# A layer's up-projection with part and remainder of x as one 512-column operand, and its products taken out of PSUM first

## The chip, the core and the metric

The kernel runs on one core of a Trainium2 chip. The metric is device time of one execution in microseconds (us); before the change it is 472.7 us, the median of three runs (472.5 to 473.08). The engines are named as the profile names them: PE is TensorE (PEld its weight loads), DVE is VectorE, ACT is ScalarE, POOL is GpSimd, SP is SyncE. PE writes its products to PSUM, from where DVE and ACT read them; everything else lives in SBUF.

## The reference

One layer (256 positions, width 1024, float32) of a mixer and a gated MLP, with a LayerNorm after each. The change touches the MLP alone, 2 x 2816 channels wide:

```python
def conv_ffn_sublayer(x, w_up, w_ffn_conv, b_ffn_conv, w_down):
    u = causal_dwconv(x @ w_up, w_ffn_conv) + b_ffn_conv
    gate, val = jnp.split(u, 2, axis=-1)
    return (jax.nn.silu(gate) * val) @ w_down

x = layer_norm(DN_ALPHA * x + mix, ln1_g, ln1_b)
ffn = conv_ffn_sublayer(x, w_up, w_ffn_conv, b_ffn_conv, w_down)
x = layer_norm(DN_ALPHA * x + ffn, ln2_g, ln2_b)
```

`causal_dwconv` is y_t = w_0 u_t + w_1 u_(t-1) + w_2 u_(t-2), channel by channel.

## The kernel before

**Products in three.** Every float32 operand of a product is split in two (`split`, L164): ACT casts it to the type in which PE multiplies (the part, `h`), DVE subtracts the part from the source (the remainder, `l`). `mm3` (L227) then makes a product of three matmuls, part by part, part by remainder and remainder by part, all summed in one PSUM tile.

**Weights as pieces.** Weights arrive in blocks of 1 MB (63 of them, `blocks`), DMAs on SP into three `raw` buffers. `prep` (L137) splits the next piece of a block, 128 x 512, into a pair (`h`, `l`) of the 61 `b2` buffers; a block is four pieces. A piece may be split as long as it is less than `LEAD` = 10 pieces beyond those that products have used up (`used`). After each group of products comes `tick(n)` (L174): it counts the `n` pieces used up, runs what was put on the list `late`, splits up to `n` + 1 pieces, then runs the group's `consume`, then one entry of the list `side`.

**The up-projection.** `project` (L238) makes two tiles of 128 channels by 256 positions from four pieces: 8 steps of the contraction, each an `mm3`, into one of three PSUM tiles named `acc` (another five are named `att`). The weights are the stationary operand, `x1Th` and `x1Tl` (part and remainder of x, turned) the moving one, 256 columns. What follows a tile is in `hidden` (L703): `taps` (L697) runs on the PSUM tile itself, first tap and bias on ACT (L699), the other two taps on DVE (L701), two instructions of which the second needs the first. For a gate tile a SiLU on ACT (L710) is put on `late`; for a value tile DVE multiplies with the gate (L714), and the split of the result into `h` and `l` is put on `late`.

**The loop.** The first pair of channel blocks (j = 0) is projected with x as the stationary operand (L734 takes it out of PSUM); `first_up` (L740), four times on `side`, turns it on PE (L743) into `att` tiles and gives it to the same `gate` and `value`; its result is `h0`. Then j = 2, 4, ..., 20 each project two gate tiles (called A and B below) and two value tiles (C and D), which are 8 pieces, and from j = 4 on also run the down-projection of the pair before, 4 pieces; j = 4 runs two, that of `h0` first. One down-projection is 18 matmuls of 512 columns and 12 of 256 (`sums`, L631: two tiles of 512 for the first 128 positions; one of 512 and two of 256 for the others).

The engines run their instructions in the order of the built program, which a scheduler makes of the order in the code.

Of the kernel before, what the change touches and what calls it, by code (L numbers as in the profile page):

```python
# [28 lines left out]
GATE = 5376  # L29

RAW = 3
LEAD = 10
B2 = 61
WARM = 6

# [2 lines left out]
def trunk(ctx: ExitStack, tc, x, w_in, w_short_conv, w_moba_proj, w_dil_proj, w_conv_proj, w_mix_out,  # L38
# [18 lines left out]
    def buf(dt=F32, shape=(P, 512)):  # L57
        return act.tile(list(shape), dt, tag="b2", name=fresh("b"), bufs=B2)

    def acc(shape=(P, 512)):  # L60
        return ps.tile(list(shape), F32, tag="acc", name=fresh("acc"), bufs=3)
# [52 lines left out]
            block(kview(w_down, 0, D, i, i + 2))  # L114

    loads, pieces, ready, loading = [], [], [], [None]
    used = [0]

    def load_next(between=None):
        i = len(loads)  # L120
# [16 lines left out]
    def prep(n=1):  # L137

        for _ in range(n):
            i = len(ready)  # L140
            if i >= min(len(pieces), used[0] + LEAD):
                return
            r, c, last = pieces[i]
            h, l = buf(F32R), buf(F32R)
            split(r[:, c:c + 512], h, l)
            ready.append((h, l))
            if last:
                load_next()

    def take(n):  # L150

        i = used[0]
        assert len(ready) >= i + n, (len(ready), i, n)
        return ready[i:i + n]
# [19 lines left out]
    def tick(n, consume=None, ahead=1):  # L174


        used[0] += n
        while late:
            late.pop(0)()
        prep(n + ahead)  # L180
        if consume:
            consume()
        if side:
            side.pop(0)()
# [27 lines left out]
    nc.gpsimd.iota(diff, pattern=[[-1, P]], base=0, channel_multiplier=1)  # L212
    nc.vector.tensor_scalar(ident, diff, 0.0, None, op0=OP.is_equal)

    xTh = act.tile([P, KT, T], F32R, tag="xTh", name="xTh")
    xTl = act.tile([P, KT, T], F32R, tag="xTl", name="xTl")

    def transpose_x(k, k1):
        p = att((P, k1 - k, T))
# [13 lines left out]
    def cut(w, k, c0, c1):  # L233

        c = (k % 2) * 256
        return [t[:, c + c0:c + c1] for t in w[k // 2]]

    def project(consume, xh=xTh, xl=xTl, ahead=1):  # L238

        w = take(4)  # L240
        for c in range(2):
            o = acc((P, T))
            for k in range(KT):
                mm3(o, *cut(w, k, c * P, c * P + P), xh[:, k, :], xl[:, k, :], k == 0, k == KT - 1)
            tick(2, lambda: consume(c, o), ahead)

    def by_tokens(xs, n, consume, ahead=1):

# [405 lines left out]


    x1 = act.tile([P, 2, D], F32, tag="xs", name="x1", bufs=2)
    x1Th = act.tile([P, KT, T], F32R, tag="xTh", name="x1Th")
    x1Tl = act.tile([P, KT, T], F32R, tag="xTl", name="x1Tl")

    def turn_x1(t, half):  # L660
        p = acc((P, 4, P))
# [41 lines left out]
    def hidden(j):  # L703
# [12 lines left out]

        return gate, value, (h, l)

    while len(ready) < used[0] + 8:
        prep()  # L720
    w = take(8)
# [18 lines left out]
    def first_up(i, c):  # L740
        o = att((P, T))
        for t in range(2):
            nc.tensor.transpose(o[:, t * P:(t + 1) * P], u[t][:, (2 * i + c) * P:(2 * i + c + 1) * P], ident)  # L743
        (gate0, value0)[i](c, o)

    side += [lambda i=i, c=c: first_up(i, c) for i in range(2) for c in range(2)]
    dn = sums()
    pend = [h0]
    for j in range(2, NJ, 2):
        gate, value, h = hidden(j)  # L750
        project(gate, x1Th, x1Tl)
        project(value, x1Th, x1Tl)
        while 2 < j < NJ - 2 and pend:
            w = take(4)
            for t in range(2):
                if t and j == NJ - 4:
                    held = (pend[0], w)
                    tick(2)
                    break
                for c0, c1, p in dn[t]:  # L760
                    for k in range(2):
                        row_products(p, pend[0], w, k, t, c0, c1, pend[0] is h0 and k == 0, False)
                tick(2)
            pend.pop(0)
        pend.append(h)
# [38 lines left out]
```

## Time and profile before

| | us |
|---|---|
| median of 3 runs | 472.7 |
| profiled execution | 472.95 |
| its span, first to last instruction | 471.2 |
| PE busy | 460.7 (98%) |
| DVE busy | 355.5 (75%) |
| ACT busy | 268.2 (57%) |

Busy time says whether an instruction was under way; matmuls overlap, each lasting longer than the distance to the next, so PE's rate is read from the starts of successive rows in the timeline. The same holds on DVE and ACT in a smaller degree: where instructions follow without waits, they start closer together than each lasts. The stage of the change is the last 185 us or so of the span, from 287 us.

### The profile page before, as it was taken

Reading aid. Unit: us, or ns where it says so; the run is one execution under the profiler, and the core shown is the slowest. Engines: PE = TensorE matmul, PEld = TensorE weight load, DVE = VectorE, ACT = ScalarE, POOL = GpSimd, SP = SyncE. Lnnn points to the kernel's source line nnn. Section 1 sums busy time; section 2 is a strip of 40 time slices with the busy share of each in tenths; the row PEclk is TensorE's granted clock in tenths of the full one; section 3 lists DMA queues with packets and bytes.
Section 4 is the critical chain, followed back from the end, with each engine's and each line's share of the span. In section 5 each row is a group of like instructions: output and inputs, shape, how many; then the busy total and the mean of one; then the engine's idle time right before and its main releaser. Section 6 shows DMA issues by size and latency. Waiting matters only on the chain.

```text
span 471.2 us, 8149 instructions
## 1 busy us (share of the span) xinstructions
PE 460.7 (98%) x3095; PEld 423.9 (90%) x3095; DVE 355.5 (75%) x756; ACT 268.2 (57%) x568; POOL 10.4 (2%) x29
## 2 busy tenths in 40 slices
PE   7999999999999999999999999999999999999993
PEld 5999898999999888888888899999999999999983
DVE  5899996868989844964487966997676786786866
ACT  3896773837577745534455235875565564664710
POOL 1100000010100000000000000000000000000000
PEclk9999999999999999999999999999999999999998
DMA  8975647354453746645664705457545636636202
GB/s 278 307 228 180 211 147 234 126 177 133 137 179 98 232 162 222 209 128 200 224 210 125 246 1 196 162 180 268 182 176 184 215 138 222 223 100 253 99 1 89
DMA packets 57738, 83.45 MB, mean 177 GB/s; under 512 B 1704, under 2 KB 41316, under 8 KB 57700
## 3 DMA queue, kind: packets, MB, share of 16 engines
q1 hardware_dynamic: 57700, 82.94, 53.0%
q8 instruction: 24, 0.39, 0.3%
q14 instruction: 14, 0.11, 0.1%
HBM read 81.89 MB, written 1.05 MB: 176 GB/s over the span
## 4 chain that ended last, share of the span: by engine, by line
PE 95%; DVE 2%; DMA 1%; issue 0%; SPq 0%; ACT 0%; DVEq 0%
PE acc L229 23%; PE acc L231 23%; PE acc L230 23%; PE att L229 7%; PE att L230 7%; PE att L231 7%; PE att L326 2%; PE att L347 1%; DMA xs<-in_x_dram 1%; PE acc L499 1%; PE att L499 1%; DVE b L169 1%; DVE b L298 0%; PE att L587 0%; PE att L222 0%
## 5 line engine op out<-in xcount | busy, mean ns | idle before, releaser
L169 DVE TENSOR_TENSOR b<-raw,b 128x512 fp32r<-128x512 f32 x300 | 193.9, 686 | 40.8 <-ACT b L168 38.7
L168 ACT CAST b<-raw 128x512 fp32r<-128x512 f32 x288 | 160.1, 618 | 2.4 <-DMA raw<-in_w_up_dram 2.1
L229 PE MATMUL acc<-x1Th,b 128*128 128x256 f32 x320 | 90.9, 284 | 0.0
L231 PE MATMUL acc<-x1Th,b 128*128 128x256 f32 x320 | 90.6, 283 | 0.0
L230 PE MATMUL acc<-x1Tl,b 128*128 128x256 f32 x320 | 90.5, 283 | 0.0
L229 PE MATMUL acc<-xTh,b 128*128 128x256 f32 x224 | 63.8, 285 | 0.4 <-DVE b L298 0.4
L231 PE MATMUL acc<-xTh,b 128*128 128x256 f32 x224 | 63.4, 283 | 0.0
L230 PE MATMUL acc<-xTl,b 128*128 128x256 f32 x224 | 63.4, 283 | 0.0
L230 PEld LDWEIGHTS acc<-x1Tl,b 128*128 128x128 f32 x320 | 61.4, 192 | 0.1
L229 PEld LDWEIGHTS acc<-x1Th,b 128*128 128x128 f32 x320 | 61.4, 192 | 0.1
L231 PEld LDWEIGHTS acc<-x1Th,b 128*128 128x128 f32 x320 | 61.4, 192 | 0.0
L701 DVE SCALAR_TENSOR_TENSOR b<-acc,fconv,b 128x255 f32<-128x255 f32 x80 | 38.4, 480 | 30.3 <-ACT b L699 29.3
L229 PE MATMUL att<-b,b 128*128 128x512 f32 (+1 forms) x170 | 59.1, 348 | 0.0
L230 PE MATMUL att<-b,b 128*128 128x512 f32 (+1 forms) x170 | 58.9, 346 | 0.0
L231 PE MATMUL att<-b,b 128*128 128x512 f32 (+1 forms) x170 | 58.7, 346 | 0.0
L229 PE MATMUL acc<-b,xTh 128*128 128x512 f32 (+1 forms) x144 | 54.8, 382 | 0.0
L230 PE MATMUL acc<-b,xTh 128*128 128x512 f32 (+1 forms) x144 | 54.4, 378 | 0.0
L231 PE MATMUL acc<-b,xTl 128*128 128x512 f32 (+1 forms) x144 | 54.4, 378 | 0.0
L229 PEld LDWEIGHTS acc<-xTh,b 128*128 128x128 f32 x224 | 42.9, 192 | 0.7 <-PE acc L231 0.6
L230 PEld LDWEIGHTS acc<-xTl,b 128*128 128x128 f32 x224 | 43.0, 192 | 0.0
L231 PEld LDWEIGHTS acc<-xTh,b 128*128 128x128 f32 x224 | 42.9, 192 | 0.0
L699 ACT ACTIVATE b<-acc,fconv 128x256 f32<-128x256 f32 x40 | 22.5, 563 | 28.6 <-PE acc L231 28.5
(118 smaller groups left out, 646.6 us busy)
## 6 DMA issues: line engine op xcount, KB each, us to landing
raw<-in_w_in_dram SPq DMA_DIRECT2D x30, 1024.0 KB, 5.4
raw<-in_w_up_dram SPq DMA_DIRECT2D x22, 1024.0 KB, 5.2
raw<-in_w_down_dram SPq DMA_DIRECT2D x11, 1024.0 KB, 5.0
raw<-in_w_mix_out_dram SPq DMA_DIRECT2D x4, 1024.0 KB, 4.8
raw<-in_w_in_dram SPq DMA_DIRECT2D x12, 256.0 KB, 5.7
raw<-in_w_conv_proj_dram SPq DMA_DIRECT2D x4, 512.0 KB, 4.8
raw<-in_w_moba_proj_dram SPq DMA_DIRECT2D x4, 512.0 KB, 5.7
xs<-in_x_dram SPq DMA_DIRECT2D x4, 256.0 KB, 5.6
```

The source lines that it names most:

```text
L168: nc.scalar.copy(h, src)
L169: nc.vector.tensor_sub(l, src, h.bitcast(F32))
L229: nc.tensor.matmul(o, ah, bh, start=first, stop=False)
L230: nc.tensor.matmul(o, ah, bl, start=False, stop=False)
L231: nc.tensor.matmul(o, al, bh, start=False, stop=last)
L326: nc.tensor.matmul(o, qt, k[i][:, a, :], start=i == 0, stop=i == 1)
L347: nc.tensor.transpose(p[:, i, :], b, ident)
L499: last = nc.tensor.matmul(o[c], w[i][:, c * P:c * P + P], xt[:, k, :], start=k + part == 0, stop=k == KT - 1 and i == 1)
L699: nc.scalar.activation(v, o, AF.Identity, bias=w[3], scale=w[0])
L701: nc.vector.scalar_tensor_tensor(v[:, j:], o[:, :T - j], w[j], v[:, j:], op0=OP.mult, op1=OP.add)
```

## The change

The tiles of part and remainder of x become one tile, `xT` (`x1T`), in which the 256 columns of each step's part are followed by the 256 of its remainder. For j = 2 to 20 `project_wide` takes the place of `project`: it multiplies the weights' part with all 512 columns in one matmul, and the weights' remainder with x's part (256 columns) into the right half of the same PSUM tile. The two halves are then summed by `summed`: ACT copies the right half to SBUF, DVE adds the left half. `taps` gets that sum in SBUF in place of the PSUM tile. In `project_wide` a tile's `consume` comes ahead of `tick`, not inside it. The lead becomes 14 pieces from the first up-projection on, and the four `first_up` on `side` are put apart by empty entries.

```diff
--- before.py
+++ after.py
@@ -29,7 +29,6 @@
 GATE = 5376
 
 RAW = 3
-LEAD = 10
 B2 = 61
 WARM = 6
 
@@ -114,7 +113,7 @@
             block(kview(w_down, 0, D, i, i + 2))
 
     loads, pieces, ready, loading = [], [], [], [None]
-    used = [0]
+    used, lead = [0], [10]
 
     def load_next(between=None):
         i = len(loads)
@@ -138,7 +137,7 @@
 
         for _ in range(n):
             i = len(ready)
-            if i >= min(len(pieces), used[0] + LEAD):
+            if i >= min(len(pieces), used[0] + lead[0]):
                 return
             r, c, last = pieces[i]
             h, l = buf(F32R), buf(F32R)
@@ -212,8 +211,8 @@
     nc.gpsimd.iota(diff, pattern=[[-1, P]], base=0, channel_multiplier=1)
     nc.vector.tensor_scalar(ident, diff, 0.0, None, op0=OP.is_equal)
 
-    xTh = act.tile([P, KT, T], F32R, tag="xTh", name="xTh")
-    xTl = act.tile([P, KT, T], F32R, tag="xTl", name="xTl")
+    xT = act.tile([P, KT, 2, T], F32R, tag="xT", name="xT")
+    xTh, xTl = xT[:, :, 0, :], xT[:, :, 1, :]
 
     def transpose_x(k, k1):
         p = att((P, k1 - k, T))
@@ -243,6 +242,26 @@
             for k in range(KT):
                 mm3(o, *cut(w, k, c * P, c * P + P), xh[:, k, :], xl[:, k, :], k == 0, k == KT - 1)
             tick(2, lambda: consume(c, o), ahead)
+
+    def project_wide(consume, xT):
+
+
+        w = take(4)
+        for c in range(2):
+            o = acc((P, 2, T))
+            f = o.rearrange("p a t -> p (a t)")
+            for k in range(KT):
+                wh, wl = cut(w, k, c * P, c * P + P)
+                nc.tensor.matmul(f, wh, xT[:, k, :, :].rearrange("p a t -> p (a t)"), start=k == 0, stop=False)
+                nc.tensor.matmul(o[:, 1, :], wl, xT[:, k, 0, :], start=False, stop=k == KT - 1)
+            consume(c, o)
+            tick(2)
+
+    def summed(o):
+        s = buf(F32, (P, T))
+        nc.scalar.copy(s, o[:, 1, :])
+        nc.vector.tensor_add(s, o[:, 0, :], s)
+        return s
 
     def by_tokens(xs, n, consume, ahead=1):
 
@@ -654,8 +673,8 @@
 
 
     x1 = act.tile([P, 2, D], F32, tag="xs", name="x1", bufs=2)
-    x1Th = act.tile([P, KT, T], F32R, tag="xTh", name="x1Th")
-    x1Tl = act.tile([P, KT, T], F32R, tag="xTl", name="x1Tl")
+    x1T = act.tile([P, KT, 2, T], F32R, tag="xT", name="x1T")
+    x1Th, x1Tl = x1T[:, :, 0, :], x1T[:, :, 1, :]
 
     def turn_x1(t, half):
         p = acc((P, 4, P))
@@ -716,6 +735,7 @@
 
         return gate, value, (h, l)
 
+    lead[0] = 14
     while len(ready) < used[0] + 8:
         prep()
     w = take(8)
@@ -743,13 +763,15 @@
             nc.tensor.transpose(o[:, t * P:(t + 1) * P], u[t][:, (2 * i + c) * P:(2 * i + c + 1) * P], ident)
         (gate0, value0)[i](c, o)
 
-    side += [lambda i=i, c=c: first_up(i, c) for i in range(2) for c in range(2)]
+    for i in range(2):
+        for c in range(2):
+            side += [lambda i=i, c=c: first_up(i, c), lambda: None]
     dn = sums()
     pend = [h0]
     for j in range(2, NJ, 2):
         gate, value, h = hidden(j)
-        project(gate, x1Th, x1Tl)
-        project(value, x1Th, x1Tl)
+        project_wide(lambda c, o: gate(c, summed(o)), x1T)
+        project_wide(lambda c, o: value(c, summed(o)), x1T)
         while 2 < j < NJ - 2 and pend:
             w = take(4)
             for t in range(2):
```

Line numbers below are those of each kernel; L228 to L230 and L167, L168 after the change are L229 to L231 and L168, L169 before it, L718 and L720 are L699 and L701, L729 is L710 and L733 is L714.

PE, the first three steps of the contraction in a tile of the up-projection (tile A of j = 2; `b679` and `b683` are parts of weights, `b680` and `b684` remainders). Before:

```order
L229 MATMUL acc725_3489<-x1Th_3065,b679_3225 128x256
L230 MATMUL acc725_3489<-x1Tl_3066,b679_3225 128x256
L231 MATMUL acc725_3489<-x1Th_3065,b680_3226 128x256
L229 MATMUL acc725_3489<-x1Th_3065,b679_3225 128x256
L230 MATMUL acc725_3489<-x1Tl_3066,b679_3225 128x256
L231 MATMUL acc725_3489<-x1Th_3065,b680_3226 128x256
L229 MATMUL acc725_3489<-x1Th_3065,b683_3284 128x256
L230 MATMUL acc725_3489<-x1Tl_3066,b683_3284 128x256
L231 MATMUL acc725_3489<-x1Th_3065,b684_3285 128x256
```

After:

```order
L255 MATMUL acc730_3497<-x1T_3064,b679_3223 128x512
L256 MATMUL acc730_3497<-x1T_3064,b680_3224 128x256
L255 MATMUL acc730_3497<-x1T_3064,b679_3223 128x512
L256 MATMUL acc730_3497<-x1T_3064,b680_3224 128x256
L255 MATMUL acc730_3497<-x1T_3064,b683_3282 128x512
L256 MATMUL acc730_3497<-x1T_3064,b684_3283 128x256
```

Of each three matmuls the first two, which have the same weights, have become one of 512 columns.

DVE, j = 2, from the last pieces ahead of tile A on (`b726` is the gate's buffer of j = 2, `b717` that of j = 0; L168 with `raw` is a piece). Before:

```order
L169 TENSOR_TENSOR b727_3515<-raw678_3223,b726_3514 128x512
L169 TENSOR_TENSOR b729_3519<-raw678_3223,b728_3518 128x512
L701 SCALAR_TENSOR_TENSOR b721_3485<-acc725_3489,fconv_113,b721_3485 128x255
L701 SCALAR_TENSOR_TENSOR b712_3476<-att731_3527,fconv_113,b712_3476 128x255
L701 SCALAR_TENSOR_TENSOR b721_3485<-acc725_3489,fconv_113,b721_3485 128x254
L701 SCALAR_TENSOR_TENSOR b712_3476<-att731_3527,fconv_113,b712_3476 128x254
L169 TENSOR_TENSOR b734_3561<-raw696_3397,b733_3560 128x512
L701 SCALAR_TENSOR_TENSOR b721_3485<-acc732_3533,fconv_113,b721_3485 128x255
L701 SCALAR_TENSOR_TENSOR b721_3485<-acc732_3533,fconv_113,b721_3485 128x254
L169 TENSOR_TENSOR b736_3565<-raw696_3397,b735_3564 128x512
L701 SCALAR_TENSOR_TENSOR b712_3476<-att737_3571,fconv_113,b712_3476 128x255
L701 SCALAR_TENSOR_TENSOR b712_3476<-att737_3571,fconv_113,b712_3476 128x254
```

After:

```order
L168 TENSOR_TENSOR b715_3479<-raw678_3221,b714_3478 128x512
L263 TENSOR_TENSOR b731_3514<-acc730_3497,b731_3514 128x256
L720 SCALAR_TENSOR_TENSOR b726_3493<-b731_3514,fconv_112,b726_3493 128x255
L720 SCALAR_TENSOR_TENSOR b726_3493<-b731_3514,fconv_112,b726_3493 128x254
L168 TENSOR_TENSOR b733_3522<-raw696_3395,b732_3521 128x512
L168 TENSOR_TENSOR b735_3526<-raw696_3395,b734_3525 128x512
L168 TENSOR_TENSOR b737_3530<-raw696_3395,b736_3529 128x512
L720 SCALAR_TENSOR_TENSOR b717_3484<-att738_3533,fconv_112,b717_3484 128x255
L263 TENSOR_TENSOR b740_3556<-acc739_3539,b740_3556 128x256
L720 SCALAR_TENSOR_TENSOR b717_3484<-att738_3533,fconv_112,b717_3484 128x254
L168 TENSOR_TENSOR b742_3565<-raw696_3395,b741_3564 128x512
L720 SCALAR_TENSOR_TENSOR b726_3493<-b740_3556,fconv_112,b726_3493 128x255
```

An addition (L263) stands ahead of each tile's two taps, the taps read its result, and three pieces follow tile A where one did. From the first piece after the wait at 288.40 us in the trace to the product (L733) that completes the first half of `h0`'s values, DVE's list now holds 44 instructions: 17 pieces, 6 additions, 17 taps, 2 products and 2 subtractions of results.

ACT, a later j, tile A to the silu of B (the gate's buffer is `b900` before and `b929` after). Before:

```order
L699 ACTIVATE b900_4557<-acc904_4561,fconv_113 128x256
L168 CAST b911_4625<-raw885_4462 128x512
L168 CAST b913_4629<-raw885_4462 128x512
L168 CAST b916_4662<-raw885_4462 128x512
L710 ACTIVATE b900_4557<-b900_4557 128x256
L699 ACTIVATE b900_4557<-acc910_4599,fconv_113 128x256
L168 CAST b918_4666<-raw885_4462 128x512
```

After:

```order
L262 COPY b934_4494<-acc933_4477 128x256
L718 ACTIVATE b929_4473<-b934_4494,fconv_112 128x256
L167 CAST b935_4501<-raw900_4321 128x512
L167 CAST b937_4505<-raw900_4321 128x512
L729 ACTIVATE b929_4473<-b929_4473 128x256
L262 COPY b941_4528<-acc940_4511 128x256
L167 CAST b942_4535<-raw913_4389 128x512
L718 ACTIVATE b929_4473<-b941_4528,fconv_112 128x256
L167 CAST b944_4539<-raw913_4389 128x512
L262 COPY b947_4560<-acc946_4543 128x256
L729 ACTIVATE b929_4473<-b929_4473 128x256
```

The copies out of PSUM (L262) are new and stand ahead of the pieces; the first tap (L718) of a tile stands behind its copy and, by what it reads, behind DVE's addition.

## Rows read from the trace of the kernel before

**Rows 1.** The page: span, and busy time of each engine.

```profile
span 471.2 us, 8149 instructions
PE 460.7 (98%) x3095; PEld 423.9 (90%) x3095; DVE 355.5 (75%) x756; ACT 268.2 (57%) x568; POOL 10.4 (2%) x29
```

**Rows 2.** The page: chain that ended last, by engine.

```profile
PE 95%; DVE 2%; DMA 1%; issue 0%; SPq 0%; ACT 0%; DVEq 0%
```

**Rows 3.** Windows: busy us (count) per engine, clock, DMA; start and a later j.

```profile
298.00:303.00 5.00, 5.00 (x44) 5.00 (x43) 5.00 (x14) 3.98 (x10) 0.00 (x0) 1.00 0.57 181
353.00:370.00 17.00, 17.00 (x128) 16.28 (x127) 12.45 (x25) 9.96 (x21) 0.00 (x0) 1.00 0.55 186
```

**Rows 4.** Groups by shape: PE, up-projection; count, busy us, mean ns, idle before.

```profile
L229 PE MATMUL acc<-x1Th,b 128*128 128x256 f32 x320 | 90.9, 284 | 0.0
```

**Rows 5.** Timeline, PE: start us, length us; first of j = 2, then 64 starts.

```profile
287.06 0.28 PE L229 MATMUL acc<-x1Th,b 128*128 128x256 f32 x1
...
299.82 0.28 PE L230 MATMUL acc<-x1Tl,b 128*128 128x256 f32 x1
...
307.50 0.28 PE L231 MATMUL acc<-x1Th,b 128*128 128x256 f32 x1
```

**Rows 6.** Timeline, PE: first and last of 204 matmuls of 512 columns.

```profile
158.33 0.40 PE L229 MATMUL acc<-b,xTh 128*128 128x512 f32 x1
...
204.51 0.40 PE L231 MATMUL acc<-b,xTl 128*128 128x512 f32 x1
```

**Rows 7.** Timeline, PE: eight of 512 columns between 256s (first of down-projection).

```profile
307.62 0.40 PE L229 MATMUL att<-b,b 128*128 128x512 f32 x1
307.85 0.40 PE L230 MATMUL att<-b,b 128*128 128x512 f32 x1
...
309.23 0.39 PE L230 MATMUL att<-b,b 128*128 128x512 f32 x1
309.46 0.28 PE L229 MATMUL acc<-x1Th,b 128*128 128x256 f32 x1
309.57 0.28 PE L230 MATMUL acc<-x1Tl,b 128*128 128x256 f32 x1
```

**Rows 8.** Timeline, DVE, start of the stage: start, length, [idle before].

```profile
288.40 3.70 DVE L169 TENSOR_TENSOR b<-raw,b 128x512 fp32r<-128x512 f32 x6 [3.99 <-ACT b L168]
292.02 0.48 DVE L701 SCALAR_TENSOR_TENSOR b<-acc,fconv,b 128x255 f32<-128x255 f32 x1
292.41 0.48 DVE L701 SCALAR_TENSOR_TENSOR b<-att,fconv,b 128x255 f32<-128x255 f32 x1
...
294.18 1.00 DVE L701 SCALAR_TENSOR_TENSOR b<-acc,fconv,b 128x255 f32<-128x255 f32 x2
296.26 0.69 DVE L169 TENSOR_TENSOR b<-raw,b 128x512 fp32r<-128x512 f32 x1 [1.08 <-ACT b L168]
...
300.55 0.75 DVE L714 TENSOR_TENSOR b<-b,b 128x256 f32<-128x256 f32 x2
...
306.86 0.42 DVE L169 TENSOR_TENSOR b<-b,b 128x256 fp32r<-128x256 f32 x1
```

**Rows 9.** Timeline, ACT, the same stretch.

```profile
290.87 0.56 ACT L699 ACTIVATE b<-acc,fconv 128x256 f32<-128x256 f32 x1
...
293.70 1.28 ACT L710 ACT_TABLE_LOAD   x1
```

**Rows 10.** Groups by shape: the nearest instructions to the added ones.

```profile
L541 ACT COPY b<-acc 128x256 f32<-128x256 f32 x4 | 1.5, 371 | 1.9 <-PE acc L231 1.9
L544 DVE TENSOR_TENSOR b<-acc,b 128x256 f32<-128x256 f32 x4 | 1.7, 420 | 1.0 <-PE acc L231 1.0
L548 DVE SCALAR_TENSOR_TENSOR b<-b,sconv,b 128x255 f32<-128x255 f32 x4 | 1.9, 484 | 0.1
L168 ACT CAST b<-b 128x256 fp32r<-128x256 f32 x26 | 10.5, 407 | 24.5 <-DVE b L714 20.8 <-DVE b L567 3.6
L168 ACT CAST b<-att 128x256 fp32r<-128x256 f32 x14 | 5.3, 377 | 23.6 <-PE att L587 21.6 <-DVE b L169 2.0
```

## Prediction

> **What bounds the kernel now.** I read the page first: PE is busy for 460.7 of the span's 471.2 us [rows 1], and the chain that ended last is PE's for 95%, with 2% for DVE [rows 2]. So the time is what PE's queue takes, plus any wait that is put into it. Then the windows, because DVE's 75% is an average [rows 1, 3]: in a later j DVE works 12.45 of 17 us, but between 298 and 303 us 5.00 of 5.00, at the start of the very stage that the change touches. TensorE's granted clock stands at 1.00 in both, its upper level, 2.4 GHz; I expect it to stay there. Last the timelines of PE, DVE and ACT, for what an instruction occupies. In the groups a matmul of 256 columns lasts 284 ns [rows 4], but successive ones start closer, and only the distance between starts can be saved.
>
> **The pair of matmuls (gain).** 64 starts of 256-column matmuls lie between 299.82 and 307.50 us: 7.68 us / 64 = 120 ns each [rows 5]. 203 starts of 512 columns lie between 158.33 and 204.51 us: 46.18 / 203 = 227.5 ns [rows 6]. Twice the columns cost 107.5 ns more, so some 12.5 ns of each matmul do not depend on its width, and those are saved with the matmul that goes. Three of 256 take 360 ns; one of 512 and one of 256 take 347.5. There are 320 such threes [rows 4]: 320 x 12.5 ns = 4.0 us. The alternation of widths is not in the trace for long. At the changes of width a 512 behind a 256 takes 0.23 us and a 256 behind a 512 0.11 [rows 7]; so the pair may be anything from 340 to 355 ns, the gain from 6.4 to 1.6 us. I take 4.0, from the long runs.
>
> The trace's fixed part can be weighed against a rule. The Trainium skill, "TensorE: Matmul & The Clock Gate", section "Back-to-back issue gap", gives N / 2.4 + 2.5 ns between warm matmuls: 109.2 ns for 256 columns and 215.8 for 512, an estimate from that page. By that rule the change would save 2.5 ns per three, 0.8 us in all. The trace does not agree: 120 and 227.5 ns at a clock of 1.00.
>
> **What is added on ACT and DVE.** Per tile one ACT copy from PSUM, 0.37 us by the same operation and shape in the mixer, and one DVE addition with a PSUM operand, 0.42 by the multiplication of that shape [rows 10]; 40 tiles, so 15 and 17 us of work. The taps on DVE then read SBUF: 484 ns [rows 10] against 0.48 now [rows 8], nothing. The first tap on ACT reads SBUF in place of PSUM: 0.56 [rows 9] plus the 30 ns by which casts of this shape differ [rows 10], 0.59; bounds 0.56 and 0.65. None of it is on PE. It costs time only where PE waits for DVE or ACT, and there are two such places to look at.
>
> **A later j (cover holds).** PE needs four tiles of 8 x 0.3475 = 2.78 us and a down-projection of 18 x 0.2275 + 12 x 0.12 = 5.54 us: 16.66 us a period, against 17.06 now. DVE occupies, from starts that follow without a wait [rows 8]: a piece (3.70 - 0.69) / 5 = 0.60, a tap 0.39, any other instruction of 256 columns 0.33. Twelve pieces 7.2, eight taps 3.1, four additions 1.3, two products and two subtractions 1.3: 12.9 us. To that come waits inside the chain, which the new order leaves bare at tiles A and C: the addition, then ACT's tap, then DVE's tap is 0.42 + 0.59 + two hand-overs of 0.04 (the two dependent taps take 1.00 us, 2 x 0.48 and 0.04 [rows 8]) = 1.09 in place of 0.33, twice 0.76; at B a piece covers all but 0.16; four instructions that wait for DVE's own result, 0.13 each; the cast of C's result, 0.58, and the cast of the piece behind it, 0.18. Together 3.0: 15.9 us. DVE fits under PE with 0.7 us to spare per period, 4%. So I cost the additions at nothing here; the cover is PE's period, and without it each j costs the excess. A piece is split 14 ahead of use, over one period of 12, and a PSUM tile is waited for only when DVE is three tiles late, so a delay of a few us is not felt at once.
>
> **The first two j (cover gone).** Here `h0`'s chain and the silu's table load come on top, and PE does not have a down-projection to give DVE time. Now DVE works from 288.40 us on [rows 8]; the last subtraction for `h0` ends at 306.86 + 0.42 = 307.28, and PE starts the first eight matmuls that need it at 307.62 [rows 7]. The margin is 0.3 us. After the change DVE has, from the same start to the product that completes the first half of `h0`, 17 pieces x 0.60 + 6 additions x 0.33 + 17 taps x 0.39 + 4 others x 0.33 = 20.2 us; the lead of 14 alone brings three of these pieces forward. The waits: the table load, 1.28 long [rows 9] and 1.08 of DVE's idle time now [rows 8], 1.2; two bare turns over ACT, 1.5; one cast turn 0.6 and the piece behind it 0.2; four own results 0.5; second waits 0.2. That is 24.4 us, so that product starts at 312.8; with its own 0.42, ACT's cast of 0.41 [rows 10] and two hand-overs the down-projection of j = 4 can start at 313.7. PE, from 287.06 [rows 5], would be there after eight tiles and the four turns of `first_up` (now 7 x 2.88 us and 0.4 up to 307.62): 287.06 + 22.24 + 0.4 = 309.7. So PE waits 4.0 us. About half falls already ahead of tile C of j = 4, which takes the PSUM tile that D of j = 2 must leave: the 29 instructions of DVE's list up to the addition for D, 13 of them pieces, take 13.7 us and waits of 4.0, to 306.1; PE is there at 287.06 + 6 x 2.78 + 0.4 = 304.1. Bounds: none of the waits on ACT left bare, 20.2 us, gives no wait on PE at all; every instruction at its full length (0.69, 0.42, 0.48) gives 28 us with the waits, 8 us of waiting.
>
> At the end one more copy and addition lie ahead of the last hidden values, behind 18 matmuls (4.1 us) of other work against a chain of some 3.7: 0, at most 0.7; I take 0.1. The DMAs are the same 1 MB loads in the same order; the larger lead only issues them earlier.
>
> **Sum.** -4.0 + 4.0 + 0.1 = +0.1 us on the profiled execution of 472.95 us, which is 0.25 above the median of 472.7. A measurement of this kernel tells about 0.2%, 0.95 us, from no change. On the median: **472.8 us**, no change that can be told.
>
> **Rivals.**
> A, the forecast: the gain is given back at the start of the stage. For it: DVE is full there already and the margin is 0.3 us. 471.9 to 473.7, chance 0.52.
> B, faster: the waits there are covered by more than I count, or the pair gains more. It decides at a DVE list under 23.4 us in place of 24.4. Against it: 20.2 us are bare occupancy. With two of the waits' four us hidden, or a pair of 341 ns, 472.8 - 2 = 470.8; with no wait on PE 468.8. Chance 0.22.
> C, slower: DVE becomes the bound of every later j. It decides where a tile costs DVE over 0.17 us more than I count (0.7 / 4). With 0.3 us more per tile the period is 17.1 in place of 16.66: over the eight j that follow +3.5, less what the lead and the PSUM tiles absorb, about 2: 472.8 + 1.5 = 474.3, up to 476. For it: the chain goes back and forth between ACT and DVE four times per j, and 4% is little. Chance 0.23.
> D, the change does not do what it says: the fixed part is not saved with the matmul (a pair at 355 to 360 ns), while the waits stay. Then the gain is 0 to 1.6 us and the time 475.2 to 476.8. Against it: both rates come from long runs. Chance 0.03. The rule of the Trainium skill named above falls into this case: by its 0.8 us the time would be 476.0.
>
> **How the numbers follow.** The likeliest case gives 472.8. Range 470.2 to 475.0: it holds A, most of B and C; outside lie B without any wait, the far end of C, and D. Faster by over 0.2% is B, 0.22, and slower C and D, 0.26; A is the rest, 0.52.
>
> **What would show it.** Starts of successive pairs in a later j 347 ns apart; PE idle near 304 to 306 us ahead of a tile, with DVE's addition as what ended it, and again at the first down-projection, ended by ACT's cast of `h0`, together about 4 us; no idle PE in later j, with DVE busy for some 14 us of each 16.66 (12.45 now [rows 3], and four additions). Wrong would be PE without gaps there (B), gaps that come back in each j, DVE busy without a pause (C), or pairs of 355 ns (D).

## Result and profile after

The changed kernel took 476.2 us (474.39 to 476.23, four executions), the kernel before 472.65 us beside it; the ratio is 1.0063, interval [1.0047, 1.0079]. The forecast was 472.8 with a range to 475.0. The time lies above the range: slower, where no change was the likeliest.

The page of the changed kernel: span and busy time of each engine, then from its groups PE's up-projection and the first matmul of each three of the down-projection (count, then busy us and mean ns, then idle before and what ended it).

```profile
span 474.1 us, 7483 instructions
PE 461.5 (97%) x2775; PEld 409.0 (86%) x2775; DVE 370.2 (78%) x796; ACT 282.0 (59%) x608; POOL 10.4 (2%) x29
...
L255 PE MATMUL acc<-x1T,b 128*128 128x512 f32 x320 | 113.7, 399 | 1.6 <-DVE b L263 1.6
L256 PE MATMUL acc<-x1T,b 128*128 128x256 f32 x320 | 89.8, 281 | 0.0
...
L228 PE MATMUL att<-b,b 128*128 128x512 f32 (+1 forms) x170 | 59.1, 348 | 1.5 <-ACT b L167 1.5
```

Against [rows 1, 4] PE has 320 matmuls fewer and is no less busy, and two idle times are new: 1.6 us ended by DVE's addition (L263, in `summed`), 1.5 ended by ACT's cast (L167). Their place stands in PE's timeline of the changed kernel (start us, length us, [idle before <- what ended it]):

```profile
305.74 0.28 PE L256 MATMUL acc<-x1T,b 128*128 128x256 f32 x1
307.67 0.50 PE L255 MATMUL acc<-x1T,b 128*128 128x512 f32 x1 [1.65 <-DVE b L263]
308.01 0.28 PE L256 MATMUL acc<-x1T,b 128*128 128x256 f32 x1
308.13 0.40 PE L255 MATMUL acc<-x1T,b 128*128 128x512 f32 x1
...
313.31 0.28 PE L256 MATMUL acc<-x1T,b 128*128 128x256 f32 x1
315.07 0.50 PE L228 MATMUL att<-b,b 128*128 128x512 f32 x1 [1.49 <-ACT b L167]
...
352.66 0.40 PE L255 MATMUL acc<-x1T,b 128*128 128x512 f32 x1
352.89 0.28 PE L256 MATMUL acc<-x1T,b 128*128 128x256 f32 x1
...
354.07 0.40 PE L255 MATMUL acc<-x1T,b 128*128 128x512 f32 x1
```

The starts 305.74 and 307.67 are 1.93 us apart, and 313.31 and 315.07 are 1.76 apart. Behind a matmul of 256 columns the next one usually starts 0.12 us later (308.01 and 308.13), so 1.81 + 1.64 = 3.4 us are lost, and some 0.1 us more at each pause, because the first matmul after it holds its successor 0.34 us off (307.67 and 308.01) where 0.24 is usual: 3.6 us in all. The first is tile C of j = 4, the second the first down-projection. In a later j four pairs take 354.07 - 352.66 = 1.41 us, 353 ns each; over the whole stage 308 pairs, those at the two waits left out, average 353.4. Three of 256 took 360 [rows 5]. So the gain is 320 x 6.6 ns = 2.1 us.

DVE, and then ACT, around the first wait, by their timelines in the changed kernel:

```profile
302.45 0.41 DVE L263 TENSOR_TENSOR b<-acc,b 128x256 f32<-128x256 f32 x1
303.53 1.00 DVE L720 SCALAR_TENSOR_TENSOR b<-b,fconv,b 128x255 f32<-128x255 f32 x2 [0.67 <-ACT b L718]
...
305.47 0.42 DVE L168 TENSOR_TENSOR b<-b,b 128x256 fp32r<-128x256 f32 x1 [0.47 <-ACT b L167]
305.99 1.29 DVE L168 TENSOR_TENSOR b<-raw,b 128x512 fp32r<-128x512 f32 x2
307.20 0.42 DVE L263 TENSOR_TENSOR b<-acc,b 128x256 f32<-128x256 f32 x1
...
314.17 0.41 DVE L733 TENSOR_TENSOR b<-b,b 128x256 f32<-128x256 f32 x1
```

```profile
302.90 0.60 ACT L718 ACTIVATE b<-b,fconv 128x256 f32<-128x256 f32 x1 [0.52 <-DVE b L263]
```

The addition that PE waits for (307.20) stands in DVE's queue behind a chain that goes over ACT twice: addition, ACT's tap, DVE's taps, product, ACT's cast, subtraction, with DVE idle for 0.67 and 0.47 us; then two pieces. Before, DVE was busy without a pause here, by the window of the kernel before (us busy and count per engine, granted clock, DMA share, GB/s; DVE's is the third, 8.90 of 8.90 us):

```profile
298.00:306.90 8.90, 8.90 (x76) 8.90 (x75) 8.90 (x22) 6.57 (x16) 0.00 (x0) 1.00 0.37 118
```

The same of the changed kernel, at the first wait and in the later j of [rows 3]:

```profile
303.00:308.00 5.00, 3.35 (x18) 2.71 (x18) 3.83 (x8) 3.47 (x8) 0.00 (x0) 1.00 0.25 84
353.00:370.00 17.00, 17.00 (x97) 14.78 (x96) 13.95 (x28) 11.53 (x25) 0.00 (x0) 1.00 0.58 186
```

In the later j PE has no gap and DVE 13.95 us of work in 17.

From the stage's first matmul to the last matmul of the kernel there are 176.42 us before (287.06 to 463.48) and 177.92 after (288.52 to 466.44): -2.1 for the pairs and +3.6 for the waits make +1.5. From the last matmul to the span's end it is 7.7 us in both. But the stage also begins 1.46 us later, and nothing ahead of it was meant to differ. Rows of PE's start, of the changed kernel and then of the one before:

```profile
6.84 0.63 PE L518 MATMUL acc<-xT,b 128*128 128x256 f32 x2
7.26 0.63 PE L518 MATMUL att<-xT,b 128*128 128x256 f32 x2
...
9.82 0.53 PE L518 MATMUL att<-xT,b 128*128 128x256 f32 x2
10.20 0.40 PE L518 MATMUL acc<-xT,b 128*128 128x256 f32 x2
10.43 0.40 PE L518 MATMUL att<-xT,b 128*128 128x256 f32 x2
```

```profile
6.36 0.40 PE L499 MATMUL acc<-xTl,b 128*128 128x256 f32 x2
6.59 0.40 PE L499 MATMUL att<-xTl,b 128*128 128x256 f32 x2
...
8.56 0.40 PE L499 MATMUL att<-xTh,b 128*128 128x256 f32 x2
```

Until 9.8 us two matmuls of 256 columns start every 0.42 to 0.43 us in the one and every 0.23 to 0.24 in the other; the same group of two comes at 9.82 and at 8.56 us. The cause is TensorE's granted clock, which has two levels, 1.2 and 2.4 GHz. The trace's first record of it, at the full level, begins at 10.12 us in the changed kernel and at 4.46 us in the one before, and where it begins the distance falls to 0.23 us (10.20 and 10.43). The column of the granted clock reads 1.00 in both stretches only because it counts a stretch without a record as full.

### The profile page after: what moved, and what is told of

The parts are those of the page before. It is cut to its first block, busy times and chain, and to the rows that moved or that the text cites. A ratio compares the mean times of both kernels' runs of the same rounds, so it can differ in the third digit from the quotient of the medians.

```text
span 474.1 us, 7483 instructions
## 1 busy us (share of the span) xinstructions
PE 461.5 (97%) x2775; PEld 409.0 (86%) x2775; DVE 370.2 (78%) x796; ACT 282.0 (59%) x608; POOL 10.4 (2%) x29
## 4 chain that ended last, share of the span: by engine, by line
PE 90%; DVE 6%; ACT 2%; issue 1%; DMA 1%; DVEq 0%; ACTq 0%
PE acc L228 15%; PE acc L230 15%; PE acc L229 15%; PE acc L255 13%; PE att L228 7%; PE att L229 7%; PE att L230 7%; PE acc L256 6%; DVE b L168 2%; PE att L345 2%; PE acc L518 1%; DVE b L720 1%; PE att L366 1%; PE att L518 1%; DMA xs<-in_x_dram 1%
## 5 line engine op out<-in xcount | busy, mean ns | idle before, releaser
L168 DVE TENSOR_TENSOR b<-raw,b 128x512 fp32r<-128x512 f32 x300 | 193.9, 684 | 40.6 <-ACT b L167 38.2
L167 ACT CAST b<-raw 128x512 fp32r<-128x512 f32 x288 | 161.2, 618 | 2.8 <-DMA raw<-in_w_up_dram 2.4
L255 PE MATMUL acc<-x1T,b 128*128 128x512 f32 x320 | 113.7, 399 | 1.6 <-DVE b L263 1.6
L256 PE MATMUL acc<-x1T,b 128*128 128x256 f32 x320 | 89.8, 281 | 0.0
L255 PEld LDWEIGHTS acc<-x1T,b 128*128 128x128 f32 x320 | 60.1, 188 | 16.3 <-DVE b L263 2.0
L228 PE MATMUL acc<-xT,b 128*128 128x256 f32 x224 | 63.8, 285 | 0.4 <-DVE b L317 0.4
L230 PE MATMUL acc<-xT,b 128*128 128x256 f32 x224 | 63.4, 283 | 0.0
L229 PE MATMUL acc<-xT,b 128*128 128x256 f32 x224 | 63.4, 283 | 0.0
L228 PE MATMUL att<-b,b 128*128 128x512 f32 (+1 forms) x170 | 59.1, 348 | 1.5 <-ACT b L167 1.5
L256 PEld LDWEIGHTS acc<-x1T,b 128*128 128x128 f32 x320 | 60.5, 189 | 0.0
L229 PE MATMUL att<-b,b 128*128 128x512 f32 (+1 forms) x170 | 58.8, 346 | 0.0
L230 PE MATMUL att<-b,b 128*128 128x512 f32 (+1 forms) x170 | 58.2, 346 | 0.0
L228 PE MATMUL acc<-b,xT 128*128 128x512 f32 (+1 forms) x144 | 54.8, 382 | 0.0
L229 PE MATMUL acc<-b,xT 128*128 128x512 f32 (+1 forms) x144 | 54.4, 378 | 0.0
L230 PE MATMUL acc<-b,xT 128*128 128x512 f32 (+1 forms) x144 | 54.4, 378 | 0.0
L720 DVE SCALAR_TENSOR_TENSOR b<-b,fconv,b 128x255 f32<-128x255 f32 x80 | 38.4, 481 | 14.1 <-ACT b L718 12.6
L228 PEld LDWEIGHTS acc<-xT,b 128*128 128x128 f32 x224 | 42.9, 192 | 0.7 <-PE acc L230 0.6
L229 PEld LDWEIGHTS acc<-xT,b 128*128 128x128 f32 x224 | 43.0, 192 | 0.0
L230 PEld LDWEIGHTS acc<-xT,b 128*128 128x128 f32 x224 | 42.9, 192 | 0.0
L228 PEld LDWEIGHTS att<-b,b 128*128 128x128 f32 x170 | 32.1, 189 | 6.4 <-ACT b L167 2.0
L230 PEld LDWEIGHTS att<-b,b 128*128 128x128 f32 x170 | 32.1, 189 | 4.1
L229 PEld LDWEIGHTS att<-b,b 128*128 128x128 f32 x170 | 32.2, 189 | 4.0
```

The source lines that it names most:

```text
L167: nc.scalar.copy(h, src)
L168: nc.vector.tensor_sub(l, src, h.bitcast(F32))
L228: nc.tensor.matmul(o, ah, bh, start=first, stop=False)
L229: nc.tensor.matmul(o, ah, bl, start=False, stop=False)
L230: nc.tensor.matmul(o, al, bh, start=False, stop=last)
L255: nc.tensor.matmul(f, wh, xT[:, k, :, :].rearrange("p a t -> p (a t)"), start=k == 0, stop=False)
```

## Experiments

The "length of the stage" below is always from its first to its last matmul, so it holds neither the start of the kernel nor its tail.

**The change once more**, with nothing edited.

> The changed kernel once more, unchanged. In its profile the clock of TensorE was at the lower level until about 10 us, in that of before only until about 4 us; from there to the start of the stage the two run 1.4 us apart, and one of its four times was 1.8 us under the other three. Theory S (the start varies from execution to execution): the times fall on two levels about 1.8 us apart, near 474.4 and 476.2, both seen among these runs, and before shows the same two levels sooner or later. Rival R (the change brings the late clock): all times near 476.2 and none of before's above 473.1.

474.85 us (474.32 to 476.68, nine executions), before 472.98 (471.85 to 474.72, 32 executions), ratio 1.0045 [1.0028, 1.0062]. This time the profiled execution (474.32 us) has the quick start, the first matmuls 0.24 us per two, and its stage is 177.95 us long, with the two pauses 1.89 and 1.76 us.

The times of either kernel lie in two groups some 1.5 us apart. In all 13 traces of this case the first record of the full clock begins either at 9.8 to 10.1 us (three traces: the change, and the runs with grouped tiles after narrow ones and with the least waiting, both below) or at 3.9 to 6.8 us (ten traces); the stage begins at 288.3 to 288.5 us in the three and at 286.5 to 287.1 us in the ten. The three are each among the slowest executions of their kernel. So the slow start is not the change's; the 1.5 us of the stage are. (No execution of the upper group of the kernel before was profiled: that it has the same cause is likely, not shown.)

**Eight 512s, then eight 256s in a tile**, in place of 512, 256, 512, 256:

```diff
             for k in range(KT):
                 wh, wl = cut(w, k, c * P, c * P + P)
                 nc.tensor.matmul(f, wh, xT[:, k, :, :]...
+            for k in range(KT):
+                wh, wl = cut(w, k, c * P, c * P + P)
                 nc.tensor.matmul(o[:, 1, :], wl, xT[:, k, 0, :]...
```

> One change to the changed kernel: within a tile, the eight matmuls of 512 columns first, then the eight of 256. In the changed kernel a pair took 353 ns where long runs of one width give 347.5. Theory W (the alternation of widths costs it): the pair falls to about 347.5 ns, 6 ns x 320 = 1.9 us less PE time, and the time falls by 1 to 1.9 us (less than 1.9 where PE then waits longer for VectorE). Rival M (a 512-column matmul with both halves of x, or into both halves of a PSUM tile, is slower by itself): 236 ns at 512 columns stays and the time is the same within 0.5 us.

474.04 us (ratio 1.0027 [1.0013, 1.0042]), the stage 177.11 us, 0.84 shorter, with the pauses as they were (1.91 and 1.84). A 512 behind a 512 starts after 230 ns, a 256 behind a 256 after 113 to 120. In the changed kernel a 512 behind a 256 takes 236 and a 256 behind a 512 takes 117. So alternating costs something, but grouping gives back only a part of what the forecast had counted on: 230 ns are left where the long runs, and the down-projections of this run, have 227. The 236 of rival M don't stay, but these 230 do, and what causes them stays open.

**Three matmuls of 256 in j = 2 and 4, the wide operand after them** (lead 14 and the empty entries stay):

```diff
-        project_wide(lambda c, o: gate(c, summed(o)), x1T)
-        project_wide(lambda c, o: value(c, summed(o)), x1T)
+        if j < 6:
+            project(gate, x1Th, x1Tl)
+            project(value, x1Th, x1Tl)
+        else:
+            project_wide(lambda c, o: gate(c, summed(o)), x1T)
+            project_wide(lambda c, o: value(c, summed(o)), x1T)
```

> One change to the changed kernel: j = 2 and 4 go through project as before (three matmuls of 256, taps on the PSUM tile), j = 6 to 20 stay wide; lead 14 and the spread of the side list stay. Theory V (VectorE's list of the first two j, with the added additions and the bare turns over ScalarE, holds PE up): of PE's 3.9 us of waits at 306 and 313 us less than 1 us is left; the pair's gain is lost on 64 of 320 pairs (0.5 us); the time falls by 2.5 to 3.4 us. Rival L (the lead of 14 and the spread side list alone hold PE up): 2 us or more of the waits stay and the time falls by under 1.5 us.

471.46 us, ratio 0.9965 [0.995, 0.998]: faster than the kernel before, 3.4 us less than the change repeated. The stage is 174.71 us long. PE's groups of this run, the first of each with no idle time ahead of it:

```profile
L255 PE MATMUL acc<-x1T,b 128*128 128x512 f32 x256 | 90.8, 399 | 0.0
...
L228 PE MATMUL att<-b,b 128*128 128x512 f32 (+1 forms) x170 | 59.1, 348 | 0.0
```

Both waits are gone with the additions of the first two j, though the larger lead is still there. (`project` also takes the products out after the pieces again; a later run does that alone and keeps the waits.) 176.42 - 256 x 6.6 ns = 174.73: what is left is the gain of 256 pairs and nothing else.

**Lead 10 throughout and no empty entries** between the turns for `h0`, the operand wide everywhere:

```diff
-    lead[0] = 14
+    lead[0] = 10
...
-            side += [lambda i=i, c=c: first_up(i, c), lambda: None]
+            side += [lambda i=i, c=c: first_up(i, c)]
```

> Two changes to the changed kernel: the lead stays at 10 pieces, and first_up stands on the side list without empty entries, as before; the wide products, the additions and consume ahead of tick stay. Theory V: three pieces fewer stand in VectorE's list ahead of h0 (1.8 us), so the waits fall from 3.9 to about 2 us and the time by 1 to 2 us. Rival L (lead and side list are the whole cause): the waits fall under 0.7 us and the time by 3 us or more.

The first pause is 0.50 us, the second gone; the stage is 175.06 us, 2.9 shorter than the change's. Yet the time is 473.81 (ratio 1.0026 [1.0009, 1.0043]): the tail from the last matmul on is 9.6 us in place of 7.7. It is the same in a later run, where it is shown. So the additions alone don't make the waits either: without the pieces of the larger lead ahead of them and with `h0`'s turns earlier, they fit, but for 0.4 us (0.50 between starts where 0.12 is usual).

**The lead alone, at the start alone**: 10 for j = 2 and 4, then 14.

```diff
-    lead[0] = 14
...
         gate, value, h = hidden(j)
+        if j == 6:
+            lead[0] = 14
```

> As the change, but the lead stays at 10 pieces for j = 2 and 4 and becomes 14 from j = 6 on. Theory P (the pieces that the larger lead brings forward in DVE's list, three of 0.60 us each = 1.8 us, are the larger part of PE's two waits at the start of the stage): the two waits, 1.89 + 1.77 = 3.7 us in the repeated change, fall to 1.9 or less, and the time to 473.0 or less (repeated change: 474.85). Theory H (the larger part is that the four turns for h0 come only at every second tick): the waits stay at 3.0 or more, the time at 474.2 to 474.9. If both are needed, 1.9 to 3.0 us of waits and 473.0 to 474.2.

472.53 us, ratio 0.9999 [0.9987, 1.001]. One pause is left, at the first down-projection:

```profile
309.29 0.28 PE L256 MATMUL acc<-x1T,b 128*128 128x256 f32 x1
310.98 0.50 PE L228 MATMUL att<-b,b 128*128 128x512 f32 x1 [1.41 <-ACT b L167]
```

1.69 us between starts, 1.6 lost in place of 3.4, and a stage of 175.66 us. As theory P had it. (Of the 2.3 us that the stage is shorter, the pauses with their successors explain 1.9; 0.3 more are at the four turns of `h0` on PE, from whose starts to the next it is 0.39 us in the change repeated and 0.11 here.)

**The empty entries alone removed**, lead 14:

> As the change, with lead 14, but without the empty entries between the four turns for h0, so that one comes at each tick. Theory P: the waits stay at 3.0 us or more and the time at 474.2 to 474.9. Theory H: the waits fall to 1.9 us or less and the time to 473.0 or less. If both are needed: in between, and each of the two runs gives about half.

474.52 us (ratio 1.0029 [1.0017, 1.0041]), the stage 178.06 us, but with one pause only, in PE's timeline:

```profile
303.91 0.28 PE L256 MATMUL acc<-x1T,b 128*128 128x256 f32 x1
306.29 0.56 PE L255 MATMUL acc<-x1T,b 128*128 128x512 f32 x1 [2.10 <-DVE b L263]
...
310.05 0.40 PE L255 MATMUL acc<-x1T,b 128*128 128x512 f32 x1
```

```profile
306.40:309.80 3.40, 3.40 (x11) 2.91 (x12) 3.40 (x10) 2.48 (x6) 0.00 (x0) 0.53 0.92 301
```

The pause is 2.38 us between starts and so costs 2.3 us in place of 3.4. But behind it the granted clock is 0.53, near the lower level of 1.2 GHz, and six pairs take 310.05 - 306.29 = 3.76 us in place of 2.12: 1.6 us more. The time came out as theory P said and for another reason: by the waits alone the lead is worth 1.8 us and the entries 1.1, about half and a third of the 3.4; the clock took the second away. (Two of the nine executions took 472.63 and 472.86 us, some 1.8 under the profiled one. Whether the clock stayed up in them no trace shows.)

**Narrow j = 2 and 4, and grouped tiles after** (the two edits above together):

> The run with three matmuls of 256 in j = 2 and 4 and the wide operand after them, and in the wide tiles the eight of 512 ahead of the eight of 256. Theory W (alternating widths costs 3 to 4 ns per pair): 256 pairs x 3.5 ns = 0.9 us under the run without the grouping (471.46), so 470.6, PE's rows 230 ns (512 behind 512) and 113 to 120 ns (256 behind 256), no wait of PE. Rival (the 0.8 us of the earlier grouped run came from the start of the stage, where the order of PE's writes changes what DVE waits for): 471.2 to 471.6.

470.12 us, ratio 0.9949 [0.9935, 0.9963]: 0.5% under the kernel before. The stage is 173.86 us, 0.85 shorter than without the grouping, 3.3 ns per pair, as theory W said. PE's timeline of a tile:

```profile
356.43 2.00 PE L255 MATMUL acc<-x1T,b 128*128 128x512 f32 x8
358.27 1.12 PE L258 MATMUL acc<-x1T,b 128*128 128x256 f32 x8
359.22 1.09 PE L255 MATMUL acc<-x1T,b 128*128 128x512 f32 x4
```

Eight of 512 in 1.84 us and eight of 256 in 0.95: 349 ns a pair, 4.4 under 353.4. The stage shows less mostly because 0.2 us come back at the last hidden values: two starts of the down-projection at 453 us are 0.30 and 0.34 us apart in place of 0.23, behind ACT's cast.

**One more copy on DVE in every wide tile**, on top of narrow j = 2 and 4:

```diff
         nc.vector.tensor_add(s, o[:, 0, :], s)
+        nc.vector.tensor_copy(buf(F32, (P, T)), o[:, 0, :])
```

> The run with three matmuls of 256 in j = 2 and 4 and the wide operand after them, and in the wide tiles one more instruction on DVE per tile, a copy of 256 columns that nothing needs: 4 x 0.33 = 1.3 us of DVE's time per later j. Theory M (DVE had 0.7 us to spare in each period of 16.8, as the prediction worked out): after some 2 us that the lead and the PSUM tiles absorb, PE waits 0.6 us in each of eight j, 2 to 3 us in all, so 473.5 to 474.5. Rival F (DVE's idle share, 2.7 of 16.8 us by the windows, can be used in full): no wait of PE in the later j, 471.2 to 471.8.

PE waits nowhere in the later j and the stage is 174.72 us long, against 174.71 without the copies. DVE's window of the later j:

```profile
353.00:370.00 17.00, 17.00 (x97) 14.74 (x96) 15.26 (x33) 11.62 (x26) 0.00 (x0) 1.00 0.57 185
```

The number of theory M did not come, but this does not decide for F, because the copies don't all come on top. DVE and ACT at tile A of a later j without the copies, then DVE with them:

```profile
358.59 0.42 DVE L263 TENSOR_TENSOR b<-acc,b 128x256 f32<-128x256 f32 x1 [0.76 <-ACT b L262]
359.68 1.00 DVE L720 SCALAR_TENSOR_TENSOR b<-b,fconv,b 128x255 f32<-128x255 f32 x2 [0.67 <-ACT b L718]
...
358.18 0.37 ACT L262 COPY b<-acc 128x256 f32<-128x256 f32 x1 [1.45 <-PE acc L256]
```

```profile
358.20 0.42 DVE L263 TENSOR_TENSOR b<-acc,b 128x256 f32<-128x256 f32 x1 [0.35 <-ACT b L262]
...
359.30 1.00 DVE L721 SCALAR_TENSOR_TENSOR b<-b,fconv,b 128x255 f32<-128x255 f32 x2 [0.34 <-ACT b L719]
```

The 0.67 us behind the addition, the same again at tile C and 0.47 behind a product are turns over ACT inside DVE's own chain. What DVE has to spare is the 0.76 us ahead of the addition, where it waits for ACT's copy and the copy for PE. In the changed kernel too it is 0.76 us in each period from 363 to 431 us: the 0.7 that the forecast saw. The copies at A and C fill half of the two turns (0.67 becomes 0.34 and 0.38), so only some 0.7 of their 1.3 us comes on top, and 0.35 us are still to spare. The time is 473.72 us all the same, for the tail is 10.7 us long. Rows from DVE's end, of the run without the copies and then of this one:

```profile
453.54 1.38 DVE L627 SCALAR_TENSOR_TENSOR r<-x,att 128x512 f32<-128x512 f32 x2 [0.68 <-PE att L230]
...
457.79 1.54 DVE L641 SCALAR_TENSOR_TENSOR r<-r,mv,bB 128x512 f32<-128x512 f32 x3
```

```profile
457.32 1.38 DVE L628 SCALAR_TENSOR_TENSOR r<-x,att 128x512 f32<-128x512 f32 x2 [3.79 <-PE att L230]
...
462.19 1.53 DVE L642 SCALAR_TENSOR_TENSOR r<-r,mv,bB 128x512 f32<-128x512 f32 x3
```

The build puts the last down-projections in another order: the first half of the tokens is complete on PE only at 457.3 in place of 453.5 us, so its norm ends at 463.7 in place of 459.3, behind PE's last matmul, and the second half's norm comes after it. The 1.9 us of the run with lead 10 come about in the same way (its first residual row is at 456.99).

**Pieces ahead of the products again**, the rest of the change as it was:

```diff
-            consume(c, o)
-            tick(2)
+            tick(2, lambda: consume(c, o))
```

> As the change, but a wide tile's products are taken out of PSUM after the splitting of pieces in its tick, as the kernel before did (the other two parts of the change stay). Theory Q (the place of the products in the tick only moves DVE's work about: its list up to h0 is as long as ever): the first wait, ahead of tile C of j = 4, grows by the three pieces that now lie ahead of tile D's addition (1.8 us, to 3.7), the second shrinks by as much (to 0 to 0.3), the sum stays at 3.5 to 4.2. The time is 474.6 to 475.2 if that is all, and up to 476.5 if a pause as long as that is followed by a stretch at the lower granted clock, as the 2.38 us pause of the run without the empty entries was (0.57 between 306.3 and 310.3 us). Rival E (products first is what keeps PE fed): both waits grow, together 5.5 us or more, and waits appear in later j.

474.52 us (ratio 1.0043 [1.0026, 1.0061]), the stage 177.97 us against 177.95.

```profile
298.39 0.38 PE L762 MATMUL att<-ident,b 128*128 128x128 f32 x2
300.95 0.47 PE L255 MATMUL acc<-x1T,b 128*128 128x512 f32 x1 [2.18 <-DVE b L262]
...
306.56 0.28 PE L256 MATMUL acc<-x1T,b 128*128 128x256 f32 x1
307.55 0.50 PE L255 MATMUL acc<-x1T,b 128*128 128x512 f32 x1 [0.71 <-DVE b L262]
```

The waits moved ahead of tiles A and C of j = 4 and the one at the first down-projection is gone. The idle times sum to 2.9 us (3.1 in the change repeated), less than theory Q expected, and the place of the first is not the one it named, but the length of the stage is the same: the third part of the change only moves the waits about.

**Wide everywhere, with the least waiting I could give it**: lead 10 for j = 2 and 4, no empty entries, grouped tiles, pieces first.

> The wide operand in all ten j, with everything beside it set as the runs so far say: lead 10 for j = 2 and 4 and 14 after, no empty entries between the turns for h0, eight 512s ahead of eight 256s in a tile, pieces ahead of the products. Theory W and P together: 320 pairs x 11 ns = 3.5 us gained and 0.5 to 2 us of waits of PE at the start, so from the stage's first matmul to the last one 173.4 to 174.9 us (before 176.42, the run with narrow j = 2 and 4 and the grouping 173.86) and a time of 469.8 to 471.3. Rival (the additions alone make DVE late by more than the four pieces give back): waits above 3 us, 472 or more.

471.23 us, ratio 0.9968 [0.9956, 0.998], the stage 174.83 us. Two pauses are left at the first down-projection, ended by ACT's cast and by DVE's subtraction of `h0`; by the distances of the starts there they cost 1.5 us:

```profile
306.07 1.02 PE L228 MATMUL att<-b,b 128*128 128x512 f32 x2 [0.36 <-ACT b L167]
307.50 0.50 PE L229 MATMUL att<-b,b 128*128 128x512 f32 x1 [0.41 <-DVE b L168]
```

So the wide operand pays in all ten j once DVE's list ahead of `h0` is short enough, but narrow j = 2 and 4 are still 1 us better: 64 pairs gain 64 x 11 ns = 0.7 us, less than the pauses cost.

**Eight 512-column matmuls in place of six ahead of the first data** (`WARM = 8`), on top of the narrow and grouped run:

> The run with narrow j = 2 and 4 and the grouping, with eight instead of six 512-column matmuls ahead of the first data. Theory S (the two groups of times of one kernel, some 1.5 us apart, come from when TensorE reaches its full rate in the first 10 us: starts 213 or 120 ns apart): PE is busy until the data is there, reaches the full rate by 6 us in every execution, and all times lie within 0.6 us of each other, at 469.9 + 0.5 for the later start of the transposes = 470.4. Rival (the two groups come from elsewhere, or the rate rises at a time of its own): times still 1.3 to 2 us apart.

470.23 us, six executions from 470.07 to 470.86, where the run without it spread from 469.69 to 471.75. PE's first row:

```profile
1.18 3.22 PE L192 MATMUL acc<-warm 128*128 128x512 bf16 x8 [1.18 <-DVE warm L187]
```

No execution is 1.3 us above the others, as theory S said. That is weak evidence: of the 19 executions of the kernel before beside it only two were in the upper group (474.42 and 474.47), so six without one may be chance, and the one trace, with the full clock from 3.89 us, is like other quick starts with six. That the two groups come from the start rests on the clock records above; that two more matmuls do away with the slow one is not shown. The median is the same within the intervals (ratio 0.9947 [0.9932, 0.9962]).

## Why the prediction was wrong

**The pair of matmuls: the step that failed.** The forecast took 347.5 ns, from long runs of one width, and wrote that the alternation of widths was not in the trace for long. It is 353.4: a 512 behind a 256 costs 236 ns, not 227.5, a 256 behind a 512 117, not 120. The gain is 2.1 us, not 4.0. The bound of 355 ns held it; the choice between the bounds was wrong. Grouping the widths gives 349 and 0.85 us back, which shows that the larger part of the error is the alternation; a 512 that starts 230 ns behind another one, not 227.5, is the rest, and why that is so stays open. With the waits of 3.6 us the stage is 1.5 us longer, where the sum had +0.1.

**The first two j: right, in place and size.** Set back by the 1.46 us of the later start, DVE's addition for tile D starts at 305.7 (forecast 306.1), the product for `h0` at 312.7 (312.8), the first down-projection at 313.6 (313.7). PE loses 3.4 us there (3.6 with the successors), not 4.0, mostly because with slower pairs it arrives later: 64 x 5.9 ns = 0.4 us. The causes named, the addition and the cast, are those that the rows name, and removing the additions removes the waits. Less right was the weight of the parts: the larger lead is worth about 1.8 us of the wait, as its three pieces of 0.60 said, but the later turns for `h0`, which I counted within DVE's list and did not price apart, another 1.1; either half of the change's start alone, the additions or the lead with the entries, costs next to nothing (0.4 us and none). The parts cost only together, and the 0.3 us of margin said so.

**A later j: right in the result and in the margin.** No gap, DVE busy 13.95 us in 17 where the text says some 14 in 16.66. What DVE has to spare per period is 0.76 us, forecast 0.7. Part of that agreement is luck: with the slower pairs the period is 16.8 us, not 16.66, so DVE's list with its waits takes some 16.1, not 15.9.

**The start: not in the forecast at all.** The profiled execution before had the quick start, that of the changed kernel the slow one, with the lower clock until 10.12 us, and so had three of its four executions by their times. Between the two profiled executions: 472.95 + 1.50 (stage) + 1.46 (start) + some 0.3 (almost all of it outside the span, of which the profile shows nothing) = 476.2. The step that the range left out is this one: with the quick start the time is inside it, as the repeated median of 474.85 is. The call was wrong there too: 1.5 us of the stage are the change's.

**Rivals.** A, the mechanism, is what happened; B and C did not. The time that D gave, 475.2 to 476.8, was met, and not by D's road: of the 12.5 ns per three 6.6 are saved. The same goes for the Trainium skill, "TensorE: Matmul & The Clock Gate", section "Back-to-back issue gap": its 2.5 ns per three would give 0.8 us and the 476.0 that the forecast named; this trace shows 6.6 ns and 2.1 us. That section gives its formula as the gap of an isolated matmul and says itself that a stream with weight loads is spaced otherwise, which the forecast left out.

## What to carry to other kernels

Price a mixed sequence from rows of the mixed sequence: if the trace before has only a few changes of width, let the slower of the bounds carry the sum (here 355 ns, for 353.4 measured). Where an engine is full for a few microseconds and the margin there is tenths of one, add up everything that the change puts into that stretch (additions, pieces brought forward, turns put back) and take it out again for that stretch alone: here narrow tiles in the first two j turned +0.4% into -0.35%, and grouping the widths made it -0.5%. Of an engine's idle time only that is spare which ends with the engine that sets the pace: here 0.76 of DVE's 2.7 us per period, the rest being waits inside its own chain. Compare stage by stage from the first to the last matmul, because the start and the tail of a kernel can each move by 1.5 us and more for other reasons than the one that is priced.

## What the runs showed that I had not expected

- TensorE's clock goes up to its full level at 3.9 to 6.8 us in ten traces and at 9.8 to 10.1 us in three, of kernels whose work up to there is nearly the same. Where matmuls of 256 columns stand ahead of that time they start every 213 ns, behind it every 120. The stage begins 1.3 to 2.0 us later in the three. The column of the granted clock doesn't tell them apart, because it reads 1.00 ahead of the first record too; the starts do. With two more matmuls ahead of the data the spread was 0.8 us in place of 2.1, six executions each, too few to tell. What decides it in a given execution stays open.
- After a pause of 2.38 us between starts the granted clock was 0.53 between 306.4 and 309.8 us, and the lower rate cost 1.6 us, nearly as much as the pause. After pauses of 2.45 us (pieces first) and 1.93 us (the change) the windows show 1.00. So the length of the pause alone doesn't decide; what does, these runs don't show.
- The order in which the build ends PE's and DVE's queues changed with edits that have nothing to do with the end, and cost 1.9 and 3.0 us of tail.
